# Gate and up of layer 0: products with z and the T4 differences on GpSimd, z ahead of the phase sums, three steps of the mixer's setup moved

## The chip, the core and the metric

The kernel runs on one NeuronCore of a Trainium2 chip. It is one program: TensorE (PE in the profile; PEld is its weight load), VectorE (DVE), ScalarE (ACT), GpSimd (POOL) and SyncE (SP), whose queue issues nearly all of the DMAs. Each engine works through its own queue in order and waits at an instruction until what it needs is done. The metric is the device time of one execution in microseconds.

## What is computed

A trunk of two layers over 1024 tokens of width 1024, in float32. Each layer is `x = x + rmsnorm(mixer(rmsnorm(x)))` and then `x = x + rmsnorm(swiglu(rmsnorm(x)))`. Layer 0 mixes with forgetting attention, layer 1 with S5, a diagonal complex state space model. The change touches the SwiGLU's first part and the preparation of S5's constants:

```python
def swiglu(h, w_gate, w_up, w_down):
    return (jax.nn.silu(h @ w_gate) * (h @ w_up)) @ w_down

# in s5_mixer: per group and state
    dt = jnp.exp(log_dt.astype(f32))[:, None]
    mag = jnp.exp(lam_re * dt)
    a_re = mag * jnp.cos(lam_im * dt)
    a_im = mag * jnp.sin(lam_im * dt)
    den = lam_re * lam_re + lam_im * lam_im
    n_re = a_re - 1.0
    z_re = (n_re * lam_re + a_im * lam_im) / den
    z_im = (a_im * lam_re - n_re * lam_im) / den
    bb_re = z_re[..., None] * b_re - z_im[..., None] * b_im
    bb_im = z_re[..., None] * b_im + z_im[..., None] * b_re
```

The S5 recurrence then runs with a, bb and c. w_gate and w_up are 1024 x 2816.

## The kernel before

Every matrix product is made of three float32r products: an operand is split into a high part (a cast on ScalarE, L822, name `ah`) and a low part (the difference on VectorE, L823, name `al`), and `h x h + h x l + l x h` is summed in PSUM. Gate and up (`gate_up`) use a Winograd form: a block of 2 x 2 needs seven products in place of eight. The activations are kept as operands B11, B21, B22 and T1, and as T2, T3, T4, which `Operands.late` makes from the held tiles `hold`: T4 is B21 - B11, one subtraction of 128x1024 for each half (L123), then the cast L128 and the low part L129. The rows of the weights are combined on VectorE to S1 to S4 (L835, L836, L841, L842).

The 2816 columns go in 11 pairs of column blocks, p = 0 to 10. A pair has 14 steps, s = 0 to 13: product s // 2 of gate (s even) and of up (s odd), 12 matmuls of 128x512 each. The products, in order: A11 B11, A12 B21, S1 T1, S2 T2, S3 T3, S4 B22, A22 T4. Behind a step stand its evacuations, such as L903, L908, L910 (copies on ScalarE) and L905, L912, L915 (sums with PSUM on VectorE), the gating L891 and L895, and the preparation of the operands of later steps. Matmuls that read T1 show as `T,ah`, those with T2 and T3 as `ops,ah`.

Raw weights come through SP into a ring of four buffers: SP's queue stands until the buffer's last reader is done. The buffers of SBUF are 38 numbered pages of 4 KB per partition; a ring is a list of pages, and a tile taken from a ring waits for the readers of the tile that had its page before.

Beside layer 0's gate and up, the constants of layer 1's S5 are made, a piece at a time: `s5_params` (with `s5_small` in it) is a generator, and `when(p, s)` tells after which steps the next piece is issued; the table `first` in `trunk` gives the steps of p = 0, 1, 2, and later p take steps 5 and 12. The pieces in order: loads of lam and dt; exp(dt); a transpose on TensorE (L1068) and exp; sine and cosine, and the loads of b (L1113, into page 34); powers of a (`cmul` from `powers`); phase sums (L1150 to L1155: 1, 2, 4 and 7 entries of 64 columns) up to 8; phase sums up to 15 and z (L1157 to L1172); bb = z b (`cmul` again: L1177 to L1182, six VectorE instructions of 128x512) and the loads of c (L1199); transposes of c's real part (L1205) and its copies (L1209); those of its imaginary part; then, for each of eight chunks, products of c, bb and powers on GpSimd (L1235 to L1239, L1296 to L1298), copies of bb (L1238, ScalarE), matmuls (L1253) and stores.

The loads of c go into the pages of b and of the six products' scratch tile, and so wait for the products. The imaginary part of b is negated (L1192) ahead of the products.

A scheduler writes out each engine's order from estimated times, with raised priority for some evacuations; an engine then keeps to the written order, however late an instruction's input is. So a late input holds up all that is written behind it.

The functions that the diff touches:

Of the kernel before, what the change touches and what calls it, by code (L numbers as in the profile page):

```python
# [9 lines left out]
F32 = mybir.dt.float32  # L10
F32R = mybir.dt.float32r
AF = mybir.ActivationFunctionType
ALU = mybir.AluOpType

P = 128
# [20 lines left out]
def f32(ap):  # L36
    return ap.bitcast(F32)
# [35 lines left out]
class Operands:  # L73
# [40 lines left out]
    def late(self, n):  # L114

        V, F = self.T.nc.vector, self.F
        pages = [[self.T.R("ops", (P, 2, 512), F32R) for _ in range(2)] for _ in range(2)]
        self.tiles[n] = pages
        for h in range(2):
            if n == "T2":  # L120
                V.tensor_add(F["B11", h], F["B11", h], F["T3", h])
            if n == "T4":
                V.tensor_sub(F["B21", h], F["B21", h], F["B11", h])  # L123
            src = F[dict(T2="B11", T3="T3", T4="B21")[n], h]
            for kh in range(2):
                s, c = src[:, 2 * kh:2 * kh + 2], slice(h * 256, h * 256 + 256)
                hi, lo = pages[0][kh][:, :, c], pages[1][kh][:, :, c]
                self.T.nc.scalar.copy(hi, s)  # L128
                V.tensor_sub(lo, s, f32(hi))  # L129
# [29 lines left out]
class Trunk:  # L159
# [883 lines left out]
    def s5_small(self):  # L1043


        nc, A, c, R = self.nc, self.A, self.cst, self.R
        V = nc.vector
        tt, ts, stt = V.tensor_tensor, V.tensor_scalar, V.scalar_tensor_tensor
# [23 lines left out]
        def tmp():  # L1072
            used[0] += 1
            return w[:, used[0] - 1]
# [5 lines left out]
        lre, lim, mre, th = L  # L1080
# [33 lines left out]
        Pre, Pim = pw[:, 0], pw[:, 1]  # L1114
# [17 lines left out]
        kk = R("s5t2", (P, 2, 16, 32))  # L1132

        def powers(X, top):
            n = 1
            while n < top:
                c_ = min(n, top - n)
                self.cmul(X[:, 0, n + 1:n + 1 + c_], X[:, 1, n + 1:n + 1 + c_], X[:, 0, 1:1 + c_], X[:, 1, 1:1 + c_],
                          X[:, 0, n:n + 1].to_broadcast([P, c_, 32]), X[:, 1, n:n + 1].to_broadcast([P, c_, 32]),
                          kk[:, 0, :c_], kk[:, 1, :c_])  # L1140
                n += c_

        yield
        powers(pw, 8)
        yield
        n, N = 1, kk.rearrange("p i n a -> p (i n a)").rearrange("p (n m) -> p n m", m=64)
        while n < 15:
            c_ = min(n, 15 - n)
# [8 lines left out]
            if n == 8:  # L1157
                yield

        z = self.z = c.tile([P, 2, 32], F32, name="z5")  # L1160
        u1, u2, u3, nre = tmp(), tmp(), tmp(), tmp()
        ar, ai = Pre[:, 1], Pim[:, 1]
        tt(u1, lre, lre, op=ALU.mult)
        tt(u2, lim, lim, op=ALU.mult)
        tt(u1, u1, u2, op=ALU.add)
        V.reciprocal(u1, u1)
        V.tensor_scalar_add(nre, ar, -1.0)
        for o, (a1, b1, a2, b2), op in ((0, (nre, lre, ai, lim), ALU.add), (1, (ai, lre, nre, lim), ALU.subtract)):
            tt(u2, a1, b1, op=ALU.mult)
            tt(u3, a2, b2, op=ALU.mult)  # L1170
            tt(u2, u2, u3, op=op)
            tt(z[:, o], u2, u1, op=ALU.mult)  # L1172
        self.pw = pw

    def cmul(self, ore, oim, xr, xi, yr, yi, k1, k2):
        tt = self.nc.vector.tensor_tensor
        tt(k1, xr, yr, op=ALU.mult)  # L1177
        tt(k2, xi, yi, op=ALU.mult)
        tt(ore, k1, k2, op=ALU.subtract)
        tt(k1, xr, yi, op=ALU.mult)  # L1180
        tt(k2, xi, yr, op=ALU.mult)
        tt(oim, k1, k2, op=ALU.add)  # L1182

    def s5_params(self):


        nc, A, R = self.nc, self.A, self.R
# [1 line left out]
        yield  # L1189

        braw, kk = self.braw, R("s5w1", (P, 2, 32, 16))
        nc.vector.tensor_scalar_mul(braw[:, 1], braw[:, 1], -1.0)  # L1192
        self.bb = R("bb", (P, 2, 32, 16))
        zr, zi = (self.z[:, i, :, None].to_broadcast([P, 32, 16]) for i in range(2))
        self.cmul(self.bb[:, 0], self.bb[:, 1], braw[:, 0], braw[:, 1], zr, zi, kk[:, 0], kk[:, 1])
        craw = [R(f"s5w{i}", (P, 8, 2, HD)) for i in range(2)]
        for i, k in enumerate(("s5_c_re", "s5_c_im")):
            for d in range(2):
# [358 lines left out]
def trunk(ctx: ExitStack, tc: tile.TileContext, A, out):  # L1557
    T = Trunk(ctx, tc, A, out)
    nc, R = T.nc, T.R
# [36 lines left out]
    for f in range(8):  # L1596
        T.plan(T.cols(A["s5_w_glu"][0], f * P)[:3] + (("glu",) * 2 if f == 0 else (None,) * 2))
        if f >= 1:
# [16 lines left out]
          o=[33, 34], x=[15, 16, 17, 18, 22, 13], y=[30, 12, 14, 31], gn=[33], wf=[34], wr=[32], fg=[19, 20, 21])  # L1615
# [30 lines left out]
    T.fox(hT, og_d, first_norm(range(4, 8), (2, 3)), OUT0)  # L1646
    xr = x0.rearrange("(p b) d -> p b d", b=8)
    R.set(hold=[28, 30, 31, 34, 36, 37], t1=[20], ah=[3, 4, 20], al=[5, 6, 21], er=[29, 32])
    first = {0: (8, 10, 12), 1: (5, 6, 8, 10, 12), 2: (5, 8, 12)}
    B = Operands(T)  # L1650
    gu = T.gate_up(B, g_d[0], T.s5_params(), lambda p, s: s in first.get(p, (5, 12)))
    end = T.out_proj(lambda tb: xr[:, tb, :], A["mix_post_gain"][0], A["ffn_pre_gain"][0], x1_d, turns, B, lambda: next(gu))
# [94 lines left out]
```

## Time and profile before

| | |
|---|---|
| Median of 3 runs | 2396.48 us (2394.59 to 2397.06) |
| The profiled execution: its time, its span | 2398.92 us, 2397.1 us |
| Mean granted TensorE clock | 0.996 |
| Busy, share of the span: PE, PEld, DVE, ACT, POOL | 98%, 81%, 70%, 50%, 19% |
| Layer 0's gate and up | from about 739 us on |

A page of the profile gives busy times of the engines, the chain of work that ended last, and groups of instructions by source line. A busy TensorE need not be at its peak: matmuls that overlap count from the first's start to the last's end, and at a lower granted clock they only last longer. In the timeline a row is the start, the length in us, the engine, the line, the operation, output<-input, shapes, and in brackets the idle time of the engine just before it with what ended it. "x2" merges two instructions. Buffer numbers are left out there, so `al` of one weight is told from another by its time.

### The profile page before, as it was taken

To read this page: it belongs to the slowest core of one execution; us is meant where nothing else is said; L and a number is where in the kernel's file an instruction comes from. 1 tells how busy PE (TensorE), PEld (TensorE's weight loads), DVE (VectorE), ACT (ScalarE), POOL (GpSimd) and SP (SyncE) were. 2 spreads that over 40 slices of the span, in tenths; PEclk is the share of its full clock that TensorE was granted. 3 is DMA by queue.
4 is the path that set the end of the run, shared out by engine and by line. 5 is a ranking of instruction groups with operands and counts; after the bars stand their busy time and mean duration, and the time that the engine had idled before them with its cause. 6 is when DMAs were issued, how large, how long until landed. Compare 5 with 4: busy or idle time off the path is not lost.

```text
span 2397.1 us, 31468 instructions
## 1 busy us (share of the span) xinstructions
PE 2348.3 (98%) x11687; PEld 1944.6 (81%) x11687; DVE 1686.6 (70%) x2687; ACT 1199.5 (50%) x2029; POOL 448.7 (19%) x425
## 2 busy tenths in 40 slices
PE   8999999999999999999999999999999999999998
PEld 6788888888788778888888879888888888888886
DVE  6867777678678966667668676853795655655867
ACT  6766677677745333344554653332463333333444
POOL 3222221223300035545520002410000000000003
PEclk9999999999999999999999999999999999999999
DMA  5121112211443444343598743533434323238874
GB/s 157 40 62 50 58 51 65 62 45 62 133 129 109 119 116 133 117 138 117 197 323 312 261 164 98 153 132 101 133 97 141 110 93 119 91 111 277 284 229 158
DMA packets 256587, 320.33 MB, mean 134 GB/s; under 512 B 34289, under 2 KB 184097, under 8 KB 256434
## 3 DMA queue, kind: packets, MB, share of 16 engines
q1 hardware_dynamic: 256434, 318.33, 41.4%
q8 instruction: 91, 1.49, 0.3%
q14 instruction: 62, 0.51, 0.1%
HBM read 240.56 MB, written 77.72 MB: 133 GB/s over the span
## 4 chain that ended last, share of the span: by engine, by line
PE 79%; DVE 11%; ACT 4%; issue 3%; POOL 2%; DMA 2%; SPq 0%; DVEq 0%; ACTq 0%; POOLq 0%
PE ps L853 30%; PE ps L973 16%; PE ps L272 7%; PE ps L273 7%; PE ps L274 7%; PE ps L615 2%; PE ps L596 2%; PE ps L558 1%; DVE ps L562 1%; PE ps L559 1%; DVE ptl L600 1%; DVE y L325 1%; ACT y L302 1%; POOL o L622 1%; DVE al L823 1%
## 5 line engine op out<-in xcount | busy, mean ns | idle before, releaser
L853 PE MATMUL ps<-B,ah 128*128 128x512 f32 x992 | 306.6, 390 | 0.8 <-DVE B L90 0.6
L973 PE MATMUL ps<-wdh,gh 128*128 128x512 f32 x616 | 241.0, 391 | 1.1 <-DVE s L895 0.6
L973 PE MATMUL ps<-wdh,gl 128*128 128x512 f32 x616 | 240.8, 391 | 1.2 <-DVE gl L254 1.2
L973 PE MATMUL ps<-wdl,gh 128*128 128x512 f32 x616 | 240.7, 391 | 0.8 <-DVE wdl L254 0.8
L853 PE MATMUL ps<-ops,ah 128*128 128x512 f32 x704 | 219.7, 393 | 2.3 <-ACT s L910 2.1
L853 PEld LDWEIGHTS ps<-B,ah 128*128 128x128 f32 x992 | 186.1, 188 | 40.9 <-DVE B L90 1.2
L272 PE MATMUL ps<-hT,wh 128*128 128x512 f32 x504 | 200.6, 398 | 1.1 <-DVE pt L436 0.6
L274 PE MATMUL ps<-hT,wl 128*128 128x512 f32 x504 | 198.3, 394 | 0.0
L273 PE MATMUL ps<-hT,wh 128*128 128x512 f32 x504 | 197.4, 392 | 0.0
L853 PE MATMUL ps<-B,al 128*128 128x512 f32 x496 | 193.0, 389 | 0.0
L253 ACT CAST gh<-gr 128x1024 fp32r<-128x1024 f32 (+1 forms) x78 | 81.1, 1040 | 163.8 <-PE ps L973 139.3
L853 PEld LDWEIGHTS ps<-ops,ah 128*128 128x128 f32 x704 | 132.1, 189 | 31.8 <-ACT s L910 2.5
L254 DVE TENSOR_TENSOR gl<-gr,gh 128x1024 fp32r<-128x1024 f32 (+1 forms) x78 | 98.1, 1259 | 80.8 <-ACT gh L253 80.7
L1698 POOL TENSOR_TENSOR y<-m,s 128x512 f32<-128x512 f32 x4 | 6.5, 1629 | 759.3 <-DVE wdl L254 754.5
L823 DVE TENSOR_TENSOR al<-raw,ah 128x1024 fp32r<-128x1024 f32 x84 | 112.4, 1339 | 45.0 <-ACT ah L822 44.7
L553 POOL TENSOR_TENSOR An<-An,cmask 128x128 f32<-128x128 f32 x128 | 78.4, 615 | 341.2 <-DVE mx L562 306.9
L600 DVE TENSOR_TENSOR ptl<-ps,pth 128x512 fp32r<-128x512 f32 x192 | 102.4, 551 | 56.6 <-ACT pth L599 56.2
L973 PEld LDWEIGHTS ps<-wdh,gh 128*128 128x128 f32 x616 | 116.3, 189 | 26.5 <-DVE s L895 1.3
L853 PE MATMUL ps<-ops,al 128*128 128x512 f32 x352 | 137.7, 391 | 0.0
L973 PEld LDWEIGHTS ps<-wdh,gl 128*128 128x128 f32 x616 | 116.1, 189 | 26.4 <-DVE gl L254 2.5
L973 PEld LDWEIGHTS ps<-wdl,gh 128*128 128x128 f32 x616 | 116.2, 189 | 25.3 <-DVE wdl L254 1.2
L822 ACT CAST ah<-raw 128x1024 fp32r<-128x1024 f32 x84 | 88.4, 1052 | 92.8 <-PE ps L853 82.6
(379 smaller groups left out, 5909.6 us busy)
## 6 DMA issues: line engine op xcount, KB each, us to landing
raw<-in_ffn_w_down_dram SPq DMA_DIRECT2D x98, 512.0 KB, 5.3
gr<-g_d SPq DMA_DIRECT2D x76, 512.0 KB, 4.5
raw<-in_ffn_w_gate_dram SPq DMA_DIRECT2D x44, 512.0 KB, 4.4
raw<-in_ffn_w_up_dram SPq DMA_DIRECT2D x44, 512.0 KB, 4.1
g_d<-s SPq DMA_DIRECT2D x66, 256.0 KB, 2.2
raw<-in_fox_w_in_dram SPq DMA_DIRECT2D x32, 512.0 KB, 4.3
g_d<-up SPq DMA_DIRECT2D x44, 256.0 KB, 3.3
g_d<-up SPq DMA_DIRECT2D x21, 512.0 KB, 3.0
```

The lines of the kernel that those rows point to most:

```text
L253: self.hcopy(h, src)
L254: self.lsub.tensor_sub(l, src, f32(h))
L272: mm(ps, lh, rh, start=start, stop=False)
L273: mm(ps, lh, rl, start=False, stop=False)
L274: mm(ps, ll, rh, start=False, stop=stop)
L553: nc.gpsimd.tensor_add(An[h][:, qs], An[h][:, qs], self.cmask)
L596: nc.tensor.transpose(p2[:, i], p[:, (g + i) * P:(g + i + 1) * P], self.ident)
L600: nc.vector.tensor_sub(dl, p2[:, 0:n], f32(dh))
L822: nc.scalar.copy(h, src)
L823: V.tensor_sub(l, src, f32(h))
L853: nc.tensor.matmul(bank, x[:, k], y, start=start and k == i == 0, stop=True, skip_group_check=True)
L973: nc.tensor.matmul(bank, x[:, j, t], y[:, j], start=start and i == 0, stop=True, skip_group_check=True)
```

## The change

- The two differences for T4 (L123, per layer) are issued on GpSimd in place of VectorE.
- z is computed ahead of the phase sums instead of behind them, and the negation of b's imaginary part with it.
- `cmul` takes an engine; the six instructions of bb = z b go to GpSimd.
- At p = 2 the three pieces (transposes of c's real part, of its imaginary part, first chunk's products) stand after steps 8, 10 and 13 instead of 5, 8 and 12.

The numbers of lines move by up to 14 between L1146 and L1183: the phase sums become L1164 to L1169, `cmul` L1178 to L1183, the negation L1159.

```diff
--- before.py
+++ after.py
@@ -120,7 +120,7 @@
             if n == "T2":
                 V.tensor_add(F["B11", h], F["B11", h], F["T3", h])
             if n == "T4":
-                V.tensor_sub(F["B21", h], F["B21", h], F["B11", h])
+                self.T.nc.gpsimd.tensor_sub(F["B21", h], F["B21", h], F["B11", h])
             src = F[dict(T2="B11", T3="T3", T4="B21")[n], h]
             for kh in range(2):
                 s, c = src[:, 2 * kh:2 * kh + 2], slice(h * 256, h * 256 + 256)
@@ -1143,6 +1143,20 @@
         yield
         powers(pw, 8)
         yield
+        z = self.z = c.tile([P, 2, 32], F32, name="z5")
+        u1, u2, u3, nre = tmp(), tmp(), tmp(), tmp()
+        ar, ai = Pre[:, 1], Pim[:, 1]
+        tt(u1, lre, lre, op=ALU.mult)
+        tt(u2, lim, lim, op=ALU.mult)
+        tt(u1, u1, u2, op=ALU.add)
+        V.reciprocal(u1, u1)
+        V.tensor_scalar_add(nre, ar, -1.0)
+        for o, (a1, b1, a2, b2), op in ((0, (nre, lre, ai, lim), ALU.add), (1, (ai, lre, nre, lim), ALU.subtract)):
+            tt(u2, a1, b1, op=ALU.mult)
+            tt(u3, a2, b2, op=ALU.mult)
+            tt(u2, u2, u3, op=op)
+            tt(z[:, o], u2, u1, op=ALU.mult)
+        nc.vector.tensor_scalar_mul(self.braw[:, 1], self.braw[:, 1], -1.0)
         n, N = 1, kk.rearrange("p i n a -> p (i n a)").rearrange("p (n m) -> p n m", m=64)
         while n < 15:
             c_ = min(n, 15 - n)
@@ -1157,23 +1171,10 @@
             if n == 8:
                 yield
 
-        z = self.z = c.tile([P, 2, 32], F32, name="z5")
-        u1, u2, u3, nre = tmp(), tmp(), tmp(), tmp()
-        ar, ai = Pre[:, 1], Pim[:, 1]
-        tt(u1, lre, lre, op=ALU.mult)
-        tt(u2, lim, lim, op=ALU.mult)
-        tt(u1, u1, u2, op=ALU.add)
-        V.reciprocal(u1, u1)
-        V.tensor_scalar_add(nre, ar, -1.0)
-        for o, (a1, b1, a2, b2), op in ((0, (nre, lre, ai, lim), ALU.add), (1, (ai, lre, nre, lim), ALU.subtract)):
-            tt(u2, a1, b1, op=ALU.mult)
-            tt(u3, a2, b2, op=ALU.mult)
-            tt(u2, u2, u3, op=op)
-            tt(z[:, o], u2, u1, op=ALU.mult)
         self.pw = pw
 
-    def cmul(self, ore, oim, xr, xi, yr, yi, k1, k2):
-        tt = self.nc.vector.tensor_tensor
+    def cmul(self, ore, oim, xr, xi, yr, yi, k1, k2, eng=None):
+        tt = (eng or self.nc.vector).tensor_tensor
         tt(k1, xr, yr, op=ALU.mult)
         tt(k2, xi, yi, op=ALU.mult)
         tt(ore, k1, k2, op=ALU.subtract)
@@ -1189,10 +1190,9 @@
         yield
 
         braw, kk = self.braw, R("s5w1", (P, 2, 32, 16))
-        nc.vector.tensor_scalar_mul(braw[:, 1], braw[:, 1], -1.0)
         self.bb = R("bb", (P, 2, 32, 16))
         zr, zi = (self.z[:, i, :, None].to_broadcast([P, 32, 16]) for i in range(2))
-        self.cmul(self.bb[:, 0], self.bb[:, 1], braw[:, 0], braw[:, 1], zr, zi, kk[:, 0], kk[:, 1])
+        self.cmul(self.bb[:, 0], self.bb[:, 1], braw[:, 0], braw[:, 1], zr, zi, kk[:, 0], kk[:, 1], nc.gpsimd)
         craw = [R(f"s5w{i}", (P, 8, 2, HD)) for i in range(2)]
         for i, k in enumerate(("s5_c_re", "s5_c_im")):
             for d in range(2):
@@ -1646,7 +1646,7 @@
     T.fox(hT, og_d, first_norm(range(4, 8), (2, 3)), OUT0)
     xr = x0.rearrange("(p b) d -> p b d", b=8)
     R.set(hold=[28, 30, 31, 34, 36, 37], t1=[20], ah=[3, 4, 20], al=[5, 6, 21], er=[29, 32])
-    first = {0: (8, 10, 12), 1: (5, 6, 8, 10, 12), 2: (5, 8, 12)}
+    first = {0: (8, 10, 12), 1: (5, 6, 8, 10, 12), 2: (8, 10, 13)}
     B = Operands(T)
     gu = T.gate_up(B, g_d[0], T.s5_params(), lambda p, s: s in first.get(p, (5, 12)))
     end = T.out_proj(lambda tb: xr[:, tb, :], A["mix_post_gain"][0], A["ffn_pre_gain"][0], x1_d, turns, B, lambda: next(gu))
```

Where the order changes, first VectorE around the split of a weight of p = 1 (`al_7442`, read by a step with T3 near 803 us), before:

```order
L1178 TENSOR_TENSOR s5t_776_7425<-pw_7409 128x32
L1170 TENSOR_TENSOR s5t_764_7311<-pw_7409,s5t_764_7311 128x32
L823 TENSOR_TENSOR al_7442<-raw_7192,ah_7441 128x1024
L1123 TENSOR_TENSOR pw_7409<-s5t_764_7311 128x32
L835 TENSOR_TENSOR S_7590<-raw_7380 128x512
L1177 TENSOR_TENSOR s5t_776_7425<-pw_7409 128x32
```

and after (`s5w_773` is b):

```order
L835 TENSOR_TENSOR S_7591<-raw_7380 128x512
L1178 TENSOR_TENSOR s5t_776_7425<-pw_7409 128x32
L1153 TENSOR_SCALAR s5t_764_7311<-pw_7409 128x32
L836 TENSOR_TENSOR S_7591<-S_7591,raw_7378 128x512
L1180 TENSOR_TENSOR pw_7409<-s5t_776_7425 128x32
L1155 TENSOR_TENSOR s5t_764_7311<-s5t_764_7311 128x32
L1159 TENSOR_SCALAR s5w_773_7410<-s5w_773_7410 128x512
L823 TENSOR_TENSOR al_7442<-raw_7192,ah_7441 128x1024
```

The sums S of the next weights and the negation of b now stand ahead of `al_7442`. SP's queue for the loads that these read, before:

```order
L1113 DMA s5w_773_7410<-in_s_b_re_dram 128x32x16
L1113 DMA s5w_773_7410<-in_s_b_im_dram 128x32x16
L932 DMA g_d<-up_6942 128x1024
L936 DMA g_d<-s_7108 128x512
L937 DMA g_d<-up_7109 128x512
L938 DMA g_d<-up_7109 128x512
L231 DMA raw_7378<-in_ffn_w_gate_dram 128x8x128
L231 DMA raw_7380<-in_ffn_w_gate_dram 128x8x128
```

and after:

```order
L231 DMA raw_7378<-in_ffn_w_gate_dram 128x8x128
L1113 DMA s5w_773_7410<-in_s_b_re_dram 128x32x16
L932 DMA g_d<-up_6942 128x1024
L936 DMA g_d<-s_7108 128x512
L937 DMA g_d<-up_7109 128x512
L938 DMA g_d<-up_7109 128x512
L231 DMA raw_7380<-in_ffn_w_gate_dram 128x8x128
L1113 DMA s5w_773_7410<-in_s_b_im_dram 128x32x16
```

One gate weight went ahead of b, and b's imaginary part behind the other. VectorE around the split of the sums S1 and S2 of up at p = 2 (`al_7690`, read by the second step with T1, near 831 us), before:

```order
L905 TENSOR_TENSOR s_7644<-s_7644,ps 128x512
L1151 TENSOR_SCALAR s5t_776_7425<-R_774_7413 128x448
L823 TENSOR_TENSOR al_7690<-S_7686,ah_7689 128x1024
L1152 TENSOR_SCALAR s5t_776_7425<-s5t_776_7425 128x448
L835 TENSOR_TENSOR S_7976<-raw_7795 128x512
L1153 SCALAR_TENSOR_TENSOR R_774_7413<-s5t_776_7425,R_774_7413 128x7x64
L905 TENSOR_TENSOR up_7645<-up_7645,ps 128x512
L1154 SCALAR_TENSOR_TENSOR R_774_7413<-s5t_776_7425,R_774_7413 128x7x64
L895 TENSOR_TENSOR s_7644<-s_7644,up_7645 128x512
L1155 TENSOR_SCALAR R_774_7413<-R_774_7413 128x7x64
L1179 TENSOR_TENSOR bb_7612<-s5w_789_7610 128x512
```

and after:

```order
L1165 TENSOR_SCALAR s5t_776_7425<-R_774_7413 128x448
L1166 TENSOR_SCALAR s5t_776_7425<-s5t_776_7425 128x448
L1167 SCALAR_TENSOR_TENSOR R_774_7413<-s5t_776_7425,R_774_7413 128x7x64
L1168 SCALAR_TENSOR_TENSOR R_774_7413<-s5t_776_7425,R_774_7413 128x7x64
L1169 TENSOR_SCALAR R_774_7413<-R_774_7413 128x7x64
L905 TENSOR_TENSOR s_7644<-s_7644,ps 128x512
L823 TENSOR_TENSOR al_7690<-S_7686,ah_7689 128x1024
L835 TENSOR_TENSOR S_7976<-raw_7785 128x512
L905 TENSOR_TENSOR up_7645<-up_7645,ps 128x512
L895 TENSOR_TENSOR s_7644<-s_7644,up_7645 128x512
```

The whole last round of phase sums now stands ahead of `al_7690`, and no product with z behind it. On GpSimd's queue the products stand ahead of the first coefficient products (L1235), and on ScalarE's queue the first copies of bb (L1238) now stand ahead of the cast for S3 and the copies L908 and L910 of p = 2.

## The prediction

> **What bounds the kernel now.** I read the busy time by stretch first. In stretches of 20 us TensorE is at 20.00 of 20 nearly throughout layer 0's gate and up; two stretches are not. The columns are the stretch, its length, PE, PEld, DVE, ACT and POOL busy, the granted clock, the DMA share and GB/s; the last row is one 5 us piece.
>
> ```profile
> 820.00:840.00 20.00, 18.44 (x81) 14.91 (x81) 19.93 (x36) 5.26 (x9) 0.00 (x0) 1.00 0.33 109
> 840.00:860.00 20.00, 16.48 (x70) 13.06 (x69) 10.71 (x13) 8.16 (x14) 7.22 (x6) 0.83 0.54 120
> 845.00:850.00 5.00, 4.29 (x14) 3.75 (x15) 2.21 (x3) 1.16 (x2) 0.00 (x0) 0.50 0.91 180
> ```
>
> VectorE is full (19.93) while TensorE loses, and the clock falls to 0.50 behind the loss. The waits of TensorE between 640 and 960 us name the three places:
>
> ```profile
> PE ps L853 <- ACT s L910: 2.1, 1, 2.1
> PE ps L853 <- DVE al L823: 1.6, 1, 1.6
> PE ps L1205 <- DMA s5w<-in_s_c_re_dram: 1.4, 1, 1.4
> ```
>
> The timeline shows their order, and what stood ahead of each (start, length, then the idle time before it and its releaser):
>
> ```profile
> 827.98 0.62 PE L853 MATMUL ps<-T,ah 128*128 128x512 f32 x2
> 830.70 0.61 PE L853 MATMUL ps<-T,ah 128*128 128x512 f32 x2
> 831.58 1.23 DVE L823 TENSOR_TENSOR al<-S,ah 128x1024 fp32r<-128x1024 f32 x1
> 832.87 0.50 PE L853 MATMUL ps<-T,al 128*128 128x512 f32 x1 [1.56 <-DVE al L823]
> 840.90 0.50 ACT L1238 COPY R<-bb 64x64 f32<-64x64 f32 x2 [2.08 <-DVE bb L1182]
> 842.38 0.58 ACT L910 COPY s<-ps 128x512 f32<-128x512 f32 x1
> 843.01 0.85 PE L853 MATMUL ps<-ops,ah 128*128 128x512 f32 x2 [2.09 <-ACT s L910]
> 845.71 1.94 PE L1205 MATMUL ps<-ident,s5w 128*128 128x128 f32 x8 [1.42 <-DMA s5w<-in_s_c_re_dram]
> ```
>
> A step of 12 matmuls takes 2.72 us (827.98 to 830.70). First loss: the second step with T1 of p = 2 waits for al_7690, which VectorE reaches late. Second: ScalarE stands at L1238 for bb, so its copy L910, which frees a bank, is late. Third: the transposes of c wait for their load. Six steps and 16 transposes (about 1.03 us for eight at full clock) lie between 827.98 and the S4 step at 854.46; they need 6 x 2.72 + 2.1 = 18.4, and took 26.5. So 8.1 us are lost here: 1.56, 2.09, 1.42, and some 2.9 to the halved clock. **That is the most that can be won**, 0.34%.
>
> **The change part by part.** *Two waits go.* The six products run on GpSimd and end (below) about 820, and ScalarE reaches L1238 at about 826, so its 2.08 and TensorE's 2.09 go. The loads of c need the SBUF buffers that the products read; these are then free, the loads stand in SP's queue behind a weight load due at about 831, and the transposes come later besides: 1.42 goes. With both, the 2.9 of slow clock goes. Together -6.4.
>
> *The first wait grows.* What counts is when VectorE ends al_7690. Rows of its timeline at the start of the backlog, of the two products ahead of al_7690, and of what followed it:
>
> ```profile
> 794.72 0.41 DVE L1192 TENSOR_SCALAR s5w<-s5w 128x512 f32<-128x512 f32 x1
> 803.38 0.69 DVE L835 TENSOR_TENSOR S<-raw 128x512 f32<-128x512 f32 x1 [2.46 <-DMA raw<-in_ffn_w_gate_dram]
> 804.88 1.22 DVE L823 TENSOR_TENSOR al<-raw,ah 128x1024 fp32r<-128x1024 f32 x1
> 819.56 0.68 DVE L1177 TENSOR_TENSOR s5w<-s5w,z 128x512 f32<-128x512 f32 x1
> 820.35 0.68 DVE L1178 TENSOR_TENSOR s5w<-s5w,z 128x512 f32<-128x512 f32 x1
> ...
> 832.72 0.41 DVE L1152 TENSOR_SCALAR s5t<-s5t 128x448 f32<-128x448 f32 x1
> 833.02 0.71 DVE L835 TENSOR_TENSOR S<-raw 128x512 f32<-128x512 f32 x1
> 833.62 0.99 DVE L1153 SCALAR_TENSOR_TENSOR R<-s5t,R 128x448 f32<-128x448 f32 x1
> 834.48 0.71 DVE L905 TENSOR_TENSOR up<-up,ps 128x512 f32<-128x512 f32 x1
> 835.08 1.00 DVE L1154 SCALAR_TENSOR_TENSOR R<-s5t,R 128x448 f32<-128x448 f32 x1
> 835.97 0.72 DVE L895 TENSOR_TENSOR s<-s,up 128x512 f32<-128x512 f32 x1
> 836.57 0.65 DVE L1155 TENSOR_SCALAR R<-R 128x448 f32<-128x448 f32 x1
> 837.08 0.73 DVE L1179 TENSOR_TENSOR bb<-s5w 128x512 f32<-128x512 f32 x1
> ```
>
> VectorE runs without a gap from 803.38 to al_7690's start at 831.58: 28.2 us. Rows overlap a little, so I cost one by the distance to the next start: 0.60 for 512 columns (833.02 to 833.62). In the new order L1159 (L1192 before) and al_7442 stand behind the S sums, so counted from L1159: 28.2 - 1.5 (803.38 to 804.88, now ahead of it) + 0.34 for L1159 + 1.14 for al_7442 - 1.2 for the two products + 2.56 for the last round of phase sums, which now stands wholly ahead (L1152 0.30, L1153 0.86, L1154 0.89, L1155 0.51) = **29.5 us** without contention.
>
> *When L1159 starts* is set by SP's queue:
>
> ```profile
> 787.13 0.37 SPq L1113 DMA_DIRECT2D s5w<-in_s_b_re_dram  x1
> 787.55 2.33 SPq L1113 DMA_DIRECT2D s5w<-in_s_b_im_dram  x1
> 795.03 1.62 SPq L231 DMA_DIRECT2D raw<-in_ffn_w_gate_dram  x2
> ```
>
> Before, b's imaginary part went out at 787.55, and its negation ran at 794.72. Now it is behind the second gate load, which landed at 803.38. The same transfers then lie ahead of its end as lay ahead of that load's end, so I take 803.4. Bounds: 800.5, if the halves of b (7.2 us from 787.55 to 794.72 with what shared it) yield some 3 us to the loads; 806, if the second half adds its own time. al_7442 then ends at about 805, 1.3 us after its step's third matmul (nine steps before 827.76, plus 0.45: 803.7). TensorE waits there; that is not added, since the later wait swallows it.
>
> *Contention.* What a product on GpSimd does to VectorE is to be seen where GpSimd works at p = 3 (below, POOL alone at 852.34, then beside VectorE, with the same lines of VectorE there, and one free of it first):
>
> ```profile
> 811.96 0.68 DVE L842 TENSOR_TENSOR raw<-raw,S 128x512 f32<-128x512 f32 x1
> 852.34 1.11 POOL L1235 TENSOR_TENSOR s5w<-cc,pw 128x512 f32<-128x512 f32 x1 [97.78 <-DVE S L836]
> 858.98 2.10 POOL L1236 TENSOR_TENSOR s5w<-cc,pw 128x512 f32<-128x512 f32 x1
> 860.14 1.49 DVE L841 TENSOR_TENSOR raw<-raw,raw 128x512 f32<-128x512 f32 x1
> 861.16 3.33 POOL L1239 TENSOR_TENSOR s5w<-s5w 64x512 f32<-64x512 f32 x2
> 861.56 1.77 DVE L842 TENSOR_TENSOR raw<-raw,S 128x512 f32<-128x512 f32 x1
> ```
>
> L842 takes 1.77 instead of 0.68, that is 1.09 more: one whole product of 1.11. L841 loses about 0.8. So a product handed to GpSimd blocks VectorE for nearly its own length, more than the 0.6 it saves there. Bounds for six: 0, if none meets a VectorE instruction that minds, and 6.7. Most of VectorE's queue at that point is sums of two SBUF tiles and small powers, few read PSUM; I take 0.85 each, between the two rows and nearer to L841: **5.1 us**. Products end then near 803.4 + 6 (z's last part) + 11 = 820.
>
> The Trainium skill, SBUF — State Buffer, section "Who interferes with whom", says that a VectorE instruction with two SBUF inputs and a GpSimd instruction that reads SBUF take one port in turn, for the whole instruction; L842's row agrees, and by that rule alone the contention would be 6.7 and the result 1.6 us later.
>
> Sum: al_7690 starts at 803.4 + 29.5 + 5.1 = 838.0, and TensorE goes on 1.29 later (831.58 to 832.87): 839.3 instead of 832.87, **+6.4**. A wait of about seven microseconds also halves the clock: a wait of 1.56 cost none, one of 2.09 with a second of 1.42 behind it cost 2.9. I take 2.9 less the 0.9 by which the eight slow transposes (1.94 for 1.03) are part of it: **+2.0**; bounds 0 and 2.9.
>
> The Trainium skill, TensorE: Matmul & The Clock Gate, section "Part 1: The HAM clock gate (the "warmup" mystery)", puts the drop behind an idle window of about 3.4 us and the return behind a busy one; here it came behind 2.09, so the measurement decides, and by the rule the term would be an estimated 1.6.
>
> *T4 on GpSimd:* minus 1.14 us on VectorE, twice in each layer, and up to 2.2 of blocking (two products' width) in its place. In layer 0:
>
> ```profile
> 768.25 1.22 DVE L123 TENSOR_TENSOR hold<-hold,hold 128x1024 f32<-128x1024 f32 x1
> 769.50 1.14 ACT L128 CAST ops<-hold 128x512 fp32r<-128x512 f32 x2 [1.18 <-DVE hold L123]
> ```
>
> The steps with T4 begin some 14 us after that cast, and VectorE's wait of 2.46 at 803.38 takes up the rest: 0. Without that cover each pair costs 1.1. *Steps moved:* the coefficient products L1235 start about 10 us later than 852.34; what they feed on TensorE is not due before this, in the chain:
>
> ```profile
> 881.82 0.98 PE ps L1253 x16
> ```
>
> They took 852.34 to 864.49, so 874 is early enough: 0, and up to 2 if not.
>
> Sum: +6.4 + 2.0 - 6.4 = **+2.0 us** against the profiled execution's 2398.92 (span 2397.1), so 2400.9; that execution is 2.4 above the median 2396.48, so in the median's terms **2398.5**.
>
> **Rivals.** *All waits go.* If b's second half lands at 801 and contention is 1.5 us, al_7690 is used at 801 + 29.5 + 1.5 + 1.3 = 833.3, 0.4 later than before, after a wait short enough to keep the clock: -6.0, 2390.5. For it: 0.68 for L842 where GpSimd rests, and PSUM readers among VectorE's work; against it: L842's 1.77. *VectorE's negation stands in the way.* If b's second half lands at 806, VectorE stands at L1159 with al_7442 and all later splits behind it; with the full 6.7 al_7690 is used at 843.5: +10.6, and +2.9 for the clock, -6.4: +7.1, 2403.6. It decides from a use after 842.1 on (832.87 + 4.8 + 6.4 - 2.0). *The products don't leave ScalarE's path*, since GpSimd, starved, ends after 830: the 2.09 stays, +4.1, 2400.6. Against it: it can take 2.1 for each product and still end by 826.
>
> **How the numbers follow.** Forecast 0.48, all waits go 0.23, negation 0.24, ScalarE still waiting 0.05. Three runs spread over 2.5 us; 0.2%, 4.8 us, is about what can be told from no change. Forecast and last rival are within it: same 0.53, faster 0.23, slower 0.24. The forecast's own range is 2394 to 2402; with both other cases reached into, 2390 to 2404.
>
> **What would show it.** Right: TensorE waits for al (L823) 5 to 8 us near 832 with a granted clock near 0.5 behind it, no wait for L910 or for c; VectorE's two-input rows near 806 to 820 at 1.1 to 1.8; L1159 preceded by idle time for a load. Wrong: a wait for al under 2.5 us (then the first rival), or VectorE's rows there at 0.68. A wait for T4's operands, or for L1253, would show a term costed at nothing.

## The result, and the profile after

The changed kernel was measured twice beside the kernel before. First: median of 7 runs 2404.24 us (2400.02 to 2406.06) against 2397.05, ratio 1.0030 (95% interval 1.0021 to 1.0039). Again, among the experiments: 11 runs, 2401.17 against 2397.07, ratio **1.0017 (1.0008 to 1.0026)**. So it is slower, by 4 to 7 us, not the same. The profiled execution is one of the first seven: it took 2404.24 us, its span 2402.5, 5.4 more than before.

The stage of the forecast first. Busy time by stretch of the changed kernel (columns as before: PE, PEld, DVE, ACT, POOL, clock, DMA share, GB/s), then TensorE's waits from 640 to 960 us:

```profile
820.00:840.00 20.00, 15.99 (x66) 12.82 (x65) 19.69 (x32) 3.26 (x6) 5.28 (x4) 0.89 0.36 118
840.00:860.00 20.00, 20.00 (x93) 16.64 (x92) 11.23 (x14) 10.11 (x16) 3.48 (x3) 0.94 0.53 132
835.00:840.00 5.00, 2.80 (x7) 2.22 (x8) 4.86 (x6) 1.02 (x3) 4.84 (x4) 0.55 0.00 0
```

```profile
PE ps L853 <- DVE al L823: 5.0, 3, 4.0
PE ps L101 <- DVE y L325: 0.7, 1, 0.7
PE ps L853 <- DVE ops L129: 0.3, 1, 0.3
PE ps L853 <- ACT s L910: 0.2, 1, 0.2
```

The loss that stood between 840 and 860 now stands ahead of 840, in one place: the waits for L910 at p = 2 (2.1) and for c (1.4) are gone, the wait for al_7690 has grown from 1.56 to 4.0, with the granted clock at 0.55 behind it. The timeline of the changed kernel, engine by engine, shows how:

```profile
796.55 0.80 SPq L1113 DMA_DIRECT2D s5w<-in_s_b_im_dram  x1
804.09 0.43 DVE L1159 TENSOR_SCALAR s5w<-s5w 128x512 f32<-128x512 f32 x1 [0.28 <-DMA s5w<-in_s_b_im_dram]
835.54 1.60 DVE L823 TENSOR_TENSOR al<-S,ah 128x1024 fp32r<-128x1024 f32 x1
837.20 0.79 PE L853 MATMUL ps<-T,al 128*128 128x512 f32 x1 [4.01 <-DVE al L823]
...
813.16 1.10 POOL L1179 TENSOR_TENSOR s5w<-s5w,z 128x512 f32<-128x512 f32 x1
834.56 1.50 POOL L1180 TENSOR_TENSOR bb<-s5w 128x512 f32<-128x512 f32 x1 [20.29 <-DVE R L1168]
839.61 1.60 POOL L1183 TENSOR_TENSOR bb<-s5w 128x512 f32<-128x512 f32 x1
...
836.10 0.24 ACT L1238 COPY R<-bb 64x64 f32<-64x64 f32 x1 [7.87 <-POOL bb L1180]
841.24 0.50 ACT L1238 COPY R<-bb 64x64 f32<-64x64 f32 x2 [4.10 <-POOL bb L1183]
```

The products did not end near 820 but at 841.2. L1180 waits 20.29 us for a phase sum, L1168, with which it shares no data: bb is page 28, and so is the scratch tile of the phase sums (rings `bb` and `s5t2` both hold that page alone). z ahead of the sums therefore can't bring bb ahead of them. ScalarE stands 12 us at L1238, more than before; TensorE doesn't feel it, since it is itself late at al_7690.

Yet this stage is not where the kernel lost. Comparing the starts of the same matmuls in the two profiled executions: the changed kernel is 1.2 us ahead at 643, 0.2 ahead at 740, 0.9 behind at 778, 1.9 at 806, 4.3 where TensorE goes on behind that wait, 6.7 at 840 with the slow clock, and **0.2 behind at 860**. From 778 to 860, all in all, it made up 0.7. It is 1.9 behind at 1700, 2.8 at 1760, 4.3 at 1790, 5.2 at the end. The losses lie around T4's differences: 2.1 us from 643 to 778 and another 1.0 up to 806 in layer 0, and 2.4 between 1700 and 1790 in layer 1. A second execution of the changed kernel lost 1.9, 1.6 and 2.1 at these places. A further 1.3 us, between 1500 and 1600, it did not lose: there the granted clock, and not the change, differs (last section).

In layer 1 TensorE's waits from 1640 to 1900 us for y and for L910 were, before (two rows) and after (three rows; the waits for L89 and L90 are the same in both):

```profile
PE ps L101 <- DVE y L325: 0.3, 2, 0.2
PE ps L853 <- ACT up L910: 0.2, 1, 0.2
```

```profile
PE ps L101 <- DVE y L325: 1.1, 3, 0.7
PE ps L853 <- ACT s L910: 0.7, 1, 0.7
PE ps L853 <- ACT up L910: 0.6, 1, 0.6
```

And what stands behind them. First out_proj, where the first half's difference is made, then gate and up with the second half's; before:

```profile
1718.35 1.21 DVE L123 TENSOR_TENSOR hold<-hold,hold 128x1024 f32<-128x1024 f32 x1
1721.04 1.23 DVE L697 TENSOR_TENSOR x<-x,y 128x1024 f32<-128x1024 f32 x1
1725.91 1.09 PE L101 MATMUL ps<-ident,y 128*128 128x128 f32 x8
...
1776.09 1.89 DVE L129 TENSOR_TENSOR ops<-hold,ops 128x512 fp32r<-128x512 f32 x3
1782.60 0.58 ACT L910 COPY s<-ps 128x512 f32<-128x512 f32 x1
1783.08 1.05 ACT L822 CAST ah<-raw 128x1024 fp32r<-128x1024 f32 x1
```

and after:

```profile
1720.37 2.39 POOL L123 TENSOR_TENSOR hold<-hold,hold 128x1024 f32<-128x1024 f32 x1 [140.95 <-DVE tt L310]
1721.93 1.91 DVE L697 TENSOR_TENSOR x<-x,y 128x1024 f32<-128x1024 f32 x1
1727.58 1.06 PE L101 MATMUL ps<-ident,y 128*128 128x128 f32 x8 [0.72 <-DVE y L325]
...
1779.19 2.40 POOL L123 TENSOR_TENSOR hold<-hold,hold 128x1024 f32<-128x1024 f32 x1 [56.43 <-DVE hold L121]
1779.57 3.77 DVE L129 TENSOR_TENSOR ops<-hold,ops 128x512 fp32r<-128x512 f32 x3
1787.65 1.05 ACT L822 CAST ah<-raw 128x1024 fp32r<-128x1024 f32 x1 [3.91 <-DVE raw L842]
1788.61 0.57 ACT L910 COPY s<-ps 128x512 f32<-128x512 f32 x1
1789.23 0.74 PE L853 MATMUL ps<-ops,ah 128*128 128x512 f32 x2 [0.68 <-ACT s L910]
```

A difference takes GpSimd 2.39 us where VectorE took 1.21, and VectorE stands still beside it: L697 takes 0.68 more, three rows L129 1.88 more. And the written order moves. In out_proj the scheduler, with L123 gone from VectorE, expects y earlier and puts its transposes four matmuls (0.9 us) ahead of where they were; y isn't that early, and TensorE waits 0.72. In gate and up a cast L822, which stood behind L910 in ScalarE's order, now stands ahead of it, waits 3.91 us for L842, and L910 is late.

### The profile page after: what moved, and what is told of

It reads as the page before. It is cut to its first block, busy times and chain, and to the rows that moved or that the text cites. A ratio compares the mean times of both kernels' runs of the same rounds, so it can differ in the third digit from the quotient of the medians.

```text
span 2402.5 us, 31478 instructions
## 1 busy us (share of the span) xinstructions
PE 2350.9 (98%) x11687; PEld 1946.4 (81%) x11687; DVE 1696.5 (71%) x2677; ACT 1198.7 (50%) x2029; POOL 472.3 (20%) x435
## 4 chain that ended last, share of the span: by engine, by line
PE 76%; DVE 13%; ACT 4%; issue 3%; DMA 2%; POOL 2%; SPq 0%; DVEq 0%; ACTq 0%; POOLq 0%
PE ps L853 27%; PE ps L973 16%; PE ps L272 7%; PE ps L273 7%; PE ps L274 7%; PE ps L615 2%; PE ps L596 2%; PE ps L558 1%; DVE ps L562 1%; DVE al L823 1%; PE ps L559 1%; DVE y L325 1%; DMA raw<-in_ffn_w_up_dram 1%; DVE ptl L600 1%; ACT y L302 1%
## 5 line engine op out<-in xcount | busy, mean ns | idle before, releaser
L823 DVE TENSOR_TENSOR al<-raw,ah 128x1024 fp32r<-128x1024 f32 x84 | 114.4, 1364 | 45.5 <-ACT ah L822 45.3
L822 ACT CAST ah<-raw 128x1024 fp32r<-128x1024 f32 x84 | 88.3, 1051 | 95.8 <-PE ps L853 87.0
L853 PE MATMUL ps<-ops,a 128*128 128x512 f32 x528 | 125.7, 391 | 0.0
```

The lines of the kernel that those rows point to most:

```text
L822: nc.scalar.copy(h, src)
L823: V.tensor_sub(l, src, f32(h))
L853: nc.tensor.matmul(bank, x[:, k], y, start=start and k == i == 0, stop=True, skip_group_check=True)
```

## The experiments

Each kernel was measured beside the kernel before on the same chip, mostly 11 runs against 15 to 33; an interval of a ratio is about 0.0009 to each side, 2.1 us.

**What carries the loss.** First T4 in layer 1 alone, on the kernel before, and the change without T4 (here and below the edits show only the lines that matter):

```diff
# T4 in layer 1 alone (kernel before; self.l1 is set in layer 1's Operands)
-                V.tensor_sub(F["B21", h], F["B21", h], F["B11", h])
+                (self.T.nc.gpsimd if self.l1 else V).tensor_sub(F["B21", h], F["B21", h], F["B11", h])
# the change without T4 (changed kernel)
-                self.T.nc.gpsimd.tensor_sub(F["B21", h], F["B21", h], F["B11", h])
+                V.tensor_sub(F["B21", h], F["B21", h], F["B11", h])
```

> The kernel before, with the T4 differences (L123) on GpSimd in layer 1 alone; layer 0 and all of the S5 preparation are as before. Theory A (the loss of the change sits where T4's differences moved, a term costed at nothing): +2 to +3.5 us against the kernel before, with TensorE waiting for y (L101, about 1 us in 3 places at the end of layer 1's out_proj) and for L910 and the low parts behind it in layer 1's gate and up (about 1.5 to 2 us). Theory B (the loss comes from the stage of the S5 preparation in layer 0, and the offsets that the trace of the changed kernel shows in layer 1 are differences between executions): within 1 us of the kernel before, and none of these waits.

> The changed kernel with L123 back on VectorE in both layers; products with z on GpSimd, z ahead of the phase sums and the moved steps stay. Theory A (T4's differences carry most of the loss): 3 to 6 us faster than the changed kernel, that is +0.5 to +3 us against the kernel before; the waits for y and for L910 in layer 1 are gone, and the stage from 738 to 860 us ends within 1.5 us of the kernel before. Theory B (the S5 preparation carries it): 5 us or more slower than the kernel before still.

T4 in layer 1: 2399.19 against 2397.41, 1.0012 (1.0003 to 1.0021), and the waits for y of 1.1 us in 3 places are there. Without T4: 2397.44, 1.0002 (0.9993 to 1.0010). Theory A holds in both as to the place, at or just under the low end of its ranges: without T4 the change is neither slower nor faster, as far as 2 us can be told.

Where in T4 it lies was tried by layer and by half (the first half's difference is made in out_proj, the second's in gate and up), each on the changed kernel by the same kind of edit (GpSimd in layer 0 only; only `if h`; only `if not h`):

> The changed kernel with T4's differences (L123) on GpSimd in layer 0 alone; in layer 1 they are on VectorE again. Without T4 the change was at +0.0 us against the kernel before, with T4 in both layers at about +7, and T4 in layer 1 alone cost +1.8. Theory A (the two layers add up): +4.5 to +6 us against the kernel before, the loss shown in layer 0 as waits for y (L101), for L129 and the low parts, and as a later load of b's imaginary part. Theory B (in layer 0 only the waits seen in the trace count, about 1.0 in out_proj and 1.1 in gate and up, and the rest is the difference between executions): +1.5 to +3 us.

> The changed kernel with only the second half's difference (the one that is computed in gate and up, at 764 and 1779 us) on GpSimd; the first half's (at 706 and 1720 us, in out_proj) is on VectorE, and the transposes of y keep their old place in TensorE's order. Theory A (part of the loss is out_proj's: TensorE reaches the moved transposes of y before VectorE has made y): the waits for y fall back to 0.3 us in layer 1 and to none in layer 0, and the kernel is 1 to 2.5 us faster than the changed one. Theory B (the loss comes from GpSimd's 2.4 us and the port in gate and up): within 1 us of the changed kernel.

> The changed kernel with only the first half's T4 difference (in out_proj, at 706 and 1720 us) on GpSimd; the second half's is on VectorE. With the second half alone the ratio to the kernel before was 1.0006, with both 1.0030, with none 1.0002. Theory A (the first half carries the rest, 0.0024): 4 to 6.5 us slower than before. Theory B (the halves only cost much together, for only then VectorE's order in the stage of the S5 preparation changes fully): 1 to 2.5 us slower, the sum of the waits for y (0.7 and 1.1).

Layer 0 alone: 2399.96, 1.0017 (1.0008 to 1.0026), theory B. Second half alone: 2399.15, 1.0006 (0.9997 to 1.0015); its waits for y fell as theory A said, and its time is 5 us under the first measurement of the change, 2 under the second. First half alone: 2398.46, 1.0006 (0.9997 to 1.0015), theory B. The layers add to a price of 0.0027, the halves to 0.0008, so the whole was measured again, both kernels on one chip:

> The changed kernel itself, beside runs of the kernel before on the same chip as the other two runs of this set. T4's price by the layers adds up to the first measurement of the change (0.0002 without T4, 0.0015 for layer 0, 0.0012 for layer 1, against 1.0030), by the halves it does not (0.0002 and twice 0.0004, 1.0010). Theory A (the layers' sum is right; the halves cost more together than apart): 1.0022 to 1.0038, 5 to 9 us slower than before. Theory B (the halves' sum is right, and the first measurement lay high): 1.0006 to 1.0018, 1.5 to 4.5 us slower.

> The changed kernel without T4 on GpSimd, again, on the same chip as the changed kernel of this set, so that T4's price is their difference. Theory A: 5 to 8 us less than the changed kernel. Theory B: 1 to 3.5 us less. Either way within 2 us of the kernel before.

The change: 2401.17, 1.0017 (1.0008 to 1.0026). Without T4: 2397.16, 1.0001 (0.9992 to 1.0010). **T4 on GpSimd costs about 4.0 us** (each of the two ratios is uncertain by 2, their difference by some 3), between the two theories' differences (the ratio itself is in B's range); with four parts each uncertain by 2 us, both earlier sums are compatible with it. The traces say where it goes. From the starts of the same matmuls, two executions with T4 against two without: 1.9 us more lost in layer 0 up to 860, and 2.4 more in layer 1 from 1700 to 1880. How the time splits between the halves is not measured to better than 2 us, but each half shows its own loss: the first alone 0.9 in out_proj in each layer (643 to 740 and 1700 to 1760), the second alone 1.1 from 740 to 778 and 1.0 up to 806 in layer 0, and 0.9 from 1760 to 1800, where 0.5 is lost without T4 too. Also, with the second half alone the waits for y fall to 0.3 in layer 1 and to none in layer 0, and with the first half alone those for L910 in layer 1 go, so each half has its own waits.

T4 has a third effect. In the execution without it:

```profile
787.04 2.30 SPq L1113 DMA_DIRECT2D s5w<-in_s_b_im_dram  x1
794.19 0.43 DVE L1159 TENSOR_SCALAR s5w<-s5w 128x512 f32<-128x512 f32 x1
834.79 0.64 PE L853 MATMUL ps<-T,al 128*128 128x512 f32 x1 [3.99 <-DVE al L823]
```

b's imaginary part goes out at 787, as in the kernel before, and L1159 runs ten microseconds earlier. So the later load of b, on which the forecast counted, comes from T4's differences, not from z. (With the second half's difference alone on GpSimd L1159 starts at 803.31, with the first's alone at 794.64.) The wait of 3.99 stands there all the same: VectorE's full stretch begins with a gate load, here at 802.73, whether b is there or not.

**The other parts, one at a time.** The moved steps alone, on the kernel before; and the change without T4 and with `cmul` on VectorE again, so that only z ahead and the moved steps stay:

```diff
# moved steps alone (kernel before)
-    first = {0: (8, 10, 12), 1: (5, 6, 8, 10, 12), 2: (5, 8, 12)}
+    first = {0: (8, 10, 12), 1: (5, 6, 8, 10, 12), 2: (8, 10, 13)}
# z ahead and moved steps (change without T4)
-        self.cmul(..., kk[:, 0], kk[:, 1], nc.gpsimd)
+        self.cmul(..., kk[:, 0], kk[:, 1])
```

> The kernel before with only the three steps at p = 2 moved to 8, 10 and 13. In the written order of ScalarE the first two copies L1238 still stand ahead of L910. Theory A (the waits are separate): the wait for c (1.42 us) and what it adds to the slow clock go, the wait for L910 (2.09) stays: 1.4 to 3 us faster than before. Theory B (the waits only move: what is late is VectorE, and each removed wait comes back at the next operand): within 1 us of the kernel before.

> The change without T4 and with the six products on VectorE as before: only z ahead of the phase sums and the moved steps stay. With the products on GpSimd the ratio was 1.0002 and TensorE waited 4.0 us for al_7690. Theory A (handing the products over relieves VectorE, 0.6 us each for those that stand ahead of al_7690): al_7690 comes 0 to 1.2 us later and the kernel is 0 to 2 us slower than with GpSimd, since four of the six stand behind al_7690 in both. Theory B (the wait is made by the products beside VectorE): al_7690 comes 1 to 2 us earlier and the kernel is 1 to 2.5 us faster.

Moved steps alone: 2395.21, 0.9989 (0.9980 to 0.9998). z ahead and moved steps: 2394.40, 0.9990 (0.9981 to 0.9999). So the moved steps gain 2.2 to 2.6 us (theory A), z's place does nothing that these runs can tell, and handing the products to GpSimd takes the gain away again (theory B): 1.0002 and 1.0001 against 0.9990, **+2.7 us**. That difference is hardly larger than its uncertainty of some 2.6 us, but the traces agree with it: the kernel with the products on VectorE had gained 2.4 us between 643 and 900, and the two executions with them on GpSimd nothing (0.16 gained, 0.15 lost). TensorE's waits from 640 to 960 us with the moved steps alone, with the products on VectorE, and with them on GpSimd (both without T4):

```profile
PE ps L853 <- ACT s L910: 2.1, 1, 2.1
PE ps L853 <- DVE al L823: 0.5, 1, 0.5
```

```profile
PE ps L853 <- ACT s L910: 2.1, 1, 2.1
PE ps L853 <- DVE al L823: 1.7, 1, 1.7
```

```profile
PE ps L853 <- DVE al L823: 4.4, 2, 4.0
PE ps L853 <- ACT up L910: 1.3, 1, 1.3
```

The wait of 2.1 for L910 is only removed where TensorE waits longer at al_7690. With the products gone from VectorE's order, the last round of phase sums moves up ahead of al_7690; with them there, most of that round stands behind it. In the last of the three traces three more rows of that round (L1166 to L1168) stand ahead, 2.1 us, and L823 and L1183 lose 1.1 beside the products; two products that are gone give back 1.2. That makes 2.0 of the 2.3 by which the wait is longer.

**What the page of bb does, and what a product costs VectorE.** The scratch of the powers and phase sums was put into a half of the tile R2 that nothing uses, with T4 on GpSimd and without:

```diff
-        kk = R("s5t2", (P, 2, 16, 32))
+        kk = R2[:, 0:512].rearrange("p (i n a) -> p i n a", i=2, n=8)
```

> The changed kernel with the scratch of the powers and phase sums in an unused half of the tile R2 instead of page 28, which bb takes next. Theory A (bb waits for the last phase sum only because it takes that page): L1180 on GpSimd starts within 5 us of L1179's end (before 822 instead of 834.6), the last product ends before 830, and ScalarE's waits of 7.87 and 4.10 us at L1238 go. Of the time: by the forecast's contention (0.85 us of VectorE for each product) TensorE goes on after the first long wait 2 to 4 us later than 837.2 and the kernel is 0 to 3 us slower than the changed one; if the products cost VectorE 0.3 us or less each, TensorE goes on between 836 and 838 and the kernel is 0 to 2 us faster than the changed one. Theory B (GpSimd is late for another reason): L1180 starts at 834 as it did.

> The changed kernel without T4 on GpSimd, and with the phase sums' scratch in R2, so that the products with z run on GpSimd at about 812 to 821 us beside VectorE's backlog. With the scratch moved and T4 on GpSimd, VectorE lost about 4 us to the six products and TensorE went on 4 us later, yet the median was that of the changed kernel. Theory A (the lost time stays lost): 2.5 to 4.5 us slower than the change without T4, that is +2.5 to +5 us against the kernel before. Theory B (it is taken back behind the stage, where other waits had stood): within 1 us of the kernel before.

With T4: 2404.56 (6 runs), 1.0031 (1.0019 to 1.0044), that is 0.3 us above the first measurement of the change and 3.4 above the second. Without: 2400.99, 1.0020 (1.0011 to 1.0029), 3.5 us slower than the change without T4, as theory A had it. Rows of GpSimd, VectorE and TensorE with T4 and the scratch moved:

```profile
814.83 1.82 POOL L1180 TENSOR_TENSOR bb<-s5w 128x512 f32<-128x512 f32 x1
816.73 1.06 POOL L1181 TENSOR_TENSOR s5w<-s5w,z 128x512 f32<-128x512 f32 x1
...
813.76 1.14 DVE L1182 TENSOR_TENSOR R<-pw 128x128 f32<-128x128 f32 x1
815.43 1.38 DVE L1183 TENSOR_TENSOR pw<-R 128x128 f32<-128x128 f32 x1
816.84 1.02 DVE L1165 TENSOR_SCALAR R<-R 128x64 f32<-128x64 f32 x1
817.90 0.96 DVE L1166 TENSOR_SCALAR R<-R 128x64 f32<-128x64 f32 x1
...
842.00 0.79 PE L853 MATMUL ps<-T,al 128*128 128x512 f32 x1 [7.56 <-DVE al L823]
```

The page was the cause (theory A): L1180 starts at 814.8 instead of 834.6, and the products end at 820.3, as the forecast had it. And the forecast's contention is there: rows of 128x128 that take 0.28 us take 1.14 and 1.38, rows of 128x64 that take 0.2 take 1.02 and 0.96. L1181, L1182, L1183, L1165, L1166 and L1168 lose 4.3 us together, 0.72 for each product, and VectorE then stands 1.50 us for a cast L822 that is late with them. TensorE goes on 4.8 us later than in the changed kernel, 4.1 of it lost behind 806 us. So the late bb had spared VectorE most of the contention. The Trainium skill, SBUF — State Buffer, section "Who interferes with whom", says that the ports that VectorE and GpSimd share are held for a whole instruction and that `tensor_scalar` can take them too, in its two-port modes; L1165 at 1.02 beside a product of 1.06 agrees.

**Is VectorE's queue the cause of the old loss?** The phase sums are needed only after gate and up. On the kernel before with the moved steps (products and T4 on VectorE, scratch in R2), they were issued later, by `issue_after` behind an L912:

```diff
# s5_small: the loop of the phase sums becomes a generator self.phases, one round a turn
# s5_params, per chunk ch
+            if 0 < ch < 5:
+                with self.tc.issue_after(self.v4.ins):     # v4: the last L912
+                    next(self.phases)
# copies of bb (L1238), a3: the last L910
-                    nc.scalar.copy(self.bs[half[i], :, gi], self.bb[half[gi], i, pr])
+                    with self.tc.issue_after(self.a3.ins):
+                        nc.scalar.copy(self.bs[half[i], :, gi], self.bb[half[gi], i, pr])
```

> Built on the kernel before, with T4 and the products on VectorE: the steps moved to 8, 10 and 13; the phase sums (L1150 to L1155, needed only after gate and up) are issued from the second chunk on and kept behind that pair's L912 in VectorE's order, their scratch lies in the unused half of R2; the copies L1238 are kept behind L910 in ScalarE's order. Theory A (what costs time between 820 and 860 us is the length of VectorE's queue ahead of al_7690 and of the products): no wait of TensorE over 1 us there, and the kernel is 5 to 8.5 us faster than before. Theory B (the limit passes to another operand, c's load or the splits of the later pairs that now share VectorE with the phase sums): 1 to 3 us faster, as the moved steps alone.

2394.25, **0.9987 (0.9978 to 0.9996)**, the lowest median here, though not to be told from the 2394.40 above: the time is theory B's. In the stage theory A holds: TensorE's waits from 640 to 960 us fall to 0.8 us in two places, and it is 8.3 us ahead of the kernel before at 860, the whole of what was lost. By 1045 it is 3.1 ahead. Of the 5.3 lost in between, 3.2 go at four chunks and 1.4 at two waits for al. The matmuls of the chunks and their weight loads, which overlap, wait 7.5 us in 9 places for GpSimd's products, against 3.1 in 5; the matmuls alone 2.6 in 2 against 0.9 in 1:

```profile
  POOL s5w L1247: 7.5, 9
```

```profile
  POOL s5w L1239: 3.1, 5
```

Three runs looked for a place where the gain is kept: the chunks' first piece after step 6 instead of 5 (`first.get(p, (6, 12))`); all sums behind the last chunk, with the copies kept back for the first chunk only; and all sums with the eighth chunk, in p = 9.

> The kernel with late phase sums, and the first piece of each chunk's pair (from p = 3 on) after step 6 instead of 5, so that the matmuls of the chunk (L1253 before, now L1261) stand one step, 2.7 us, later in TensorE's order. With late sums TensorE was 8.3 us ahead at 860 us and only 3 at 1045, waiting 7.5 us in 9 places for GpSimd's L1239 (3.1 in 5 in the kernel before). Theory A (GpSimd's chain of the chunks takes the gain back): these waits fall under 2 us and the kernel is 5 to 8 us faster than before. Theory B (the gain is lost elsewhere, or the chain only moves on): within 1 us of the kernel with late sums, 2 to 4 us faster than before.

> The kernel with late phase sums, all of them behind the last chunk (VectorE at the last pair) and the copies L1238 kept behind L910 only for the first chunk; T4 and products on VectorE, steps at 8, 10 and 13. Theory A (with the sums among the chunks, VectorE and GpSimd held each other up and made the matmuls of the chunks late): TensorE's waits at those matmuls fall from 7.5 us to 3 to 4.5, and the kernel is 4.5 to 8 us faster than before. Theory B (the chain of a chunk is limited by SP's queue, and TensorE, once ahead, waits for it whatever VectorE does): 2 to 4 us faster, as with the sums among the chunks.

> As the kernel with the sums last, but the phase sums stand with the eighth chunk, behind L912 of p = 9, so that they are through before the last pair's VectorE work, on which the first matmuls of the down projection wait (9.8 us for L895 in the run before). Theory A (the 8 us won at 860 are kept until the sums run, and they cost the chunks of two pairs at most): 4.5 to 7.5 us faster than before, TensorE's wait for L895 under 2 us. Theory B (the gain is taken back wherever VectorE does the sums, since their 10 us are simply missing there): 1 to 3.5 us faster.

Later chunk matmuls: 2406.26 (5 runs), 1.0043 (1.0030 to 1.0055). The waits at the chunks go, but TensorE now waits up to 4.5 us for al, and VectorE's L835 4.87 for a load of weights. In SP's queue those loads wait 48.6 us in all for a free buffer, against 9.2 in the kernel before; the store L1257 of the chunks, which stands ahead of some of them, waits 74.1 for GpSimd, no more than in the kernel before (L1249 there, 81.6). What made the loads late is not shown. Both theories were wrong. Sums last: 2399.00, 1.0008 (0.9999 to 1.0016): TensorE keeps 7.2 us until 1085, and waits 2.9 us in 4 places at the chunks, weight loads counted as above, which is just under theory A's 3 to 4.5, and then loses all in one wait at the first matmuls of the down projection:

```profile
1193.30 0.79 PE L973 MATMUL ps<-wdh,gh 128*128 128x512 f32 x1 [9.77 <-DVE s L895]
```

Sums in p = 9: 2395.35, 0.9993 (0.9984 to 1.0002): 7.8 us kept until 1085, 2.6 at 1165, behind a wait of 3.3 for al. Theory B by the time: in all of these runs 5 us or more were taken back behind 860. That the sums did it is shown in the last two, where rounds of the sums stand directly ahead of the L895 and the al that TensorE waits for; in the run with later chunk matmuls it is not.

## Why the prediction was wrong

**The step that failed is "T4 on GpSimd: 0".** It was costed by its cover in layer 0's gate and up, where T4's steps begin 14 us later, and by VectorE's idle 2.46 us. It measured about 4.0 us. Three things were left out. The first half's difference isn't made in gate and up but in out_proj, where L697 and y are on TensorE's path. In layer 1 no 2.46 us of idle time follow, and the blocking that the prediction named (up to 2.2; L129 shows 1.88) lands on L842 and by it on ScalarE's order. And moving an instruction to another engine changes the order that the scheduler writes on all of them: y's transposes, a cast ahead of L910, b's load behind a gate load. That last move stood in the prediction, but as part of the stage, not of T4. With the T4 term at 4.0 its sum of +2.0 becomes +6.0, between the two measurements of +4.1 and +7.2; the time in the median's terms is 2402.5. That the miss is no larger is luck: the stage came out better than forecast by about half of what T4 came out worse.

**The rest of the sum**, +2.0, measured as the change without T4: +0.0 and +0.1 us. Its parts:

- *L1159 at 803.4*: 804.09. Right. That b's load would come later was right of the change, though not for the reason given, and the wait doesn't hang on it: without T4 L1159 ran at 794.19 and the wait was the same.
- *29.5 us of queue*: from L1159 to al_7690 31.45 us passed, 2.0 more than without contention, not 5.1; L1181 and L1182 beside the two products show 1.1 of it. The price for a product (0.85) was near the 0.72 that the moved scratch showed; wrong was the number of products that meet the backlog, two instead of six, because of page 28. TensorE went on at 837.20, not 839.3: +4.3 and not +6.4. It had come there 1.9 us late, so the wait itself grew by 2.4, with T4 and without.
- *Products end near 820, ScalarE's 2.08 goes*: wrong. They end at 841.2. TensorE's 2.09 went for another reason: TensorE was later than ScalarE.
- *c's wait of 1.42 goes*: right, and the moved steps alone do it: worth 2.2 to 2.6 us with what it saves of slow clock. This was the only part of the change for which a gain was measured.
- *Slow clock +2.0*: a clock of 0.55 and 0.77 in the two stretches of 5 us from 835, and 2.3 us more lag from there to 840; near in size. That was partly luck, since another execution of the same kernel, with a wait of 3.9, shows 1.5 (last section).
- *Moved steps 0*: L1253's waits from 860 on are 0.6 us against 0.9. Right.

From 806 to 860 us the changed kernel made up 1.7 us, and without T4 0.7 and 0.9 in two executions, where the forecast had +2.0; by 900, counted from 806, the latter two stood at 0.0 and -0.2. So the stage came out some 2 us better than forecast. The rivals: "all waits go" is out, since a wait of 4.0 stood there. "The negation stands in the way" had the right sign, but by another mechanism and place. "ScalarE still waiting for bb" had the right mechanism for GpSimd's lateness (though starved by a page, not by the port) and the wrong effect.

## What to carry to other kernels

Before an instruction is moved to another engine, list every place where it runs (each half, each layer), and compare the written order of all engines and of the DMA queue there; the cover in one place says nothing of the others. An operation that is moved forward in the program gains nothing while its output page is still read by something later: look for tiles that share a page. GpSimd helped nowhere in this kernel: beside a VectorE without idle time each product took back 0.72 us where it saved 0.60.

## What the runs showed of the hardware

- One difference of 128x1024 on GpSimd (2.39 to 2.72 us) held up VectorE for 1.88 us in layer 1. Even rows of 64 columns, 0.2 us by themselves, waited out a product: 1.02 and 0.96.
- What the clock loses does not follow from the length of the wait. Two executions of the change without T4, each with the wait of 3.99 us for al_7690; first stretches of 5 us from 835, then from 830 in the other:

```profile
835.00:840.00 5.00, 5.00 (x16) 3.93 (x16) 4.38 (x4) 1.53 (x3) 4.84 (x4) 0.66 0.14 32
840.00:845.00 5.00, 5.00 (x24) 4.14 (x23) 2.79 (x3) 3.10 (x6) 0.42 (x1) 1.00 1.08 219
```

```profile
830.00:835.00 5.00, 2.04 (x9) 1.34 (x8) 4.93 (x8) 0.63 (x1) 0.01 (x1) 0.91 0.11 33
835.00:840.00 5.00, 3.97 (x9) 3.17 (x10) 4.37 (x4) 1.54 (x3) 4.84 (x4) 0.50 0.01 2
840.00:845.00 5.00, 5.00 (x21) 4.05 (x20) 3.25 (x4) 3.09 (x6) 1.63 (x1) 0.91 0.97 206
```

The first lost 0.34 of 5 us, 1.7 us of full clock, the second 0.68, or 3.4, some of it inside the wait. A single wait of 2.10 (the moved steps alone: 0.80 and 0.86) cost 1.7, one of 7.56 (0.81 and 0.51) 3.4, and the kernel before, with 2.09 and 1.42, 3.4 (0.85, 0.50 and 0.97). The same is seen where the change touches nothing: behind 2370 us the kernel before shows 0.76 and 0.55, the change without T4 1.00 and 1.00 in one execution, whose matmuls run 3.1 us earlier from there on; between 1545 and 1560 the kernel before lost 1.7 (0.66 in one stretch) and the changed one 3.4 (0.88, 0.50 and 0.93).
- Medians of the same kernel beside the same reference, on two occasions, differed by 3.1 us. At this size a ratio needs more than seven runs, and parts that are measured apart need not add up.
